# Copying block (1,1) out of PSUM on ScalarE in the pooled and gate quads of a two-layer hybrid backbone

## The chip, the cores and the metric

The kernel runs on one core of a Trainium2 chip. The metric is the device time of one execution in microseconds (us). The engines are called as in the profile: PE (TensorE matmul), PEld (its weight load), DVE (VectorE), ACT (ScalarE), POOL (GpSimd) and SP (SyncE, which issues the DMAs). L1514 is line 1514 of the kernel before.

## What is computed

A latent stream `x` of 1024 tokens of width 1024 goes through two layers and a final RMSNorm. The even layer joins a convolution branch with a bidirectional recurrent branch; the change does not touch it. The odd layer is a multi-scale pooling mixer, and in it lies everything that follows:

```python
def odd_mixer(h, p, on_grid):
    z = h @ p["w_in"]
    u, g = jnp.split(z, [W_POOL], axis=-1)          # W_POOL = 2048
    ...
    d = multiscale_pool(u.reshape(bn * rows, GRID_W, W_POOL)).reshape(bn, n, W_POOL)
    d = d.reshape(bn, n, N_POOL_GROUPS, POOL_GROUP_DIM)
    y = jnp.einsum("bngi,gij->bngj", d, p["w_grp"]).reshape(bn, n, W_POOL) * p["scale"]
    return (y * jax.nn.silu(g)) @ p["w_out"]
```

`multiscale_pool` takes, in rows of 64 tokens, the mean over a window of 2, 4, 8 or 16 tokens (one window for each quarter of the channels) and subtracts the token itself. Since pooling acts along the tokens and `w_grp` along the channels, the kernel folds `w_grp` into the input weights beforehand and pools the product.

## The kernel before

The matrix products of the odd layer are made as **quads**: two row tiles of 128 output channels by two column tiles of 512 tokens, so four blocks (i, h), where i is the row tile and h the column tile. A quad needs seven products in place of eight, in the manner of Strassen. Each product is 12 matmuls (`prod`, L1013): four slices of the contraction by three passes (high weight by high data L1018, high by low L1020, low by high L1021), since each fp32 operand is split into a high and a low part. The seven weight operands of a quad are made while the quad before runs (`wquad_steps`, L979): DVE makes sums of weight blocks, and `split` (L102) makes the high part with a cast on ACT (L103) and then the low part with a subtraction on DVE (L104). In the order of the work they are wq_1, wq_5, wq_6, wq_2, wq_7, wq_3, wq_4; between wq_7 and wq_3 stands a subtraction on DVE (L1006) that wq_3 needs.

`quad` (L1031) uses three accumulators in PSUM, `qa`, `qc` and `qb`, from a pool of four. Its steps:

- p1 into `qa`; ACT copies `qa` to `qb` (L1036); p5 into `qc`, which ACT keeps as a part (L1064); p6 on top of `qb`, kept as a part as well; p2 completes `qa`, which is block (0,0).
- p7 on top of `qb`: with the part of `qc` this gives block (1,1), whose call is `put(1, 1, b, 1)`.
- p3 completes `qc`: with the part of `qb` this gives block (0,1), the second call with part 1, `put(0, 1, c, 1)`.
- p4 completes `qb` as block (1,0). p4 can start only when block (1,1) has been read out of `qb`.

The first argument of `put` is the i of `to_tokens` and `to_gate`, the second is their h. So the call with i = 1 and part 1 is the one that reads `qb` between p7 and p4, and the call with i = 0 and part 1 reads `qc`.

The stage of the change is the loop over pairs of row tiles, m = 0, 2, ..., 14 (808 to 1121 us of the span). Each pass runs a **pooled quad** (its names end in v; blocks go through `to_tokens` into padded token tiles `vp`, which `pool`, L1405, then works on in DVE) and a **gate quad** (names end in g; blocks go through `to_gate` into `y`, get a SiLU on ACT, L1527, and are multiplied with the pooled tokens on DVE, L1557). The window is 4 tokens for m = 0 and 2, 16 for m = 4 and 6, 8 for m = 8 and 10, and 2 for m = 12 and 14; `pool` does one pass of additions (L1420) for each doubling. The blocks of `y` and DVE's sums of them (L962 to L966) are stored to device memory (L1448) and loaded again (L1467) as the operands of the output projection, whose quads end in wo and follow from 1111 us on.

In a pooled quad both blocks with part 1 are read from PSUM by one DVE addition (L1514). In a gate quad this is so too (L1525), but for block (1,1) of the last pair (m = 14): there ACT copies `qb` to `y` (L1523), and DVE adds in place.

The order of instructions on each engine is found by the scheduler, which simulates the program's time; evictions (`put` and L1036) stand under a raised priority. Instructions of one engine run in the order that it wrote down.

Of the kernel before, what the change touches and what calls it, by code (L numbers as in the profile page):

```python
# [56 lines left out]
def body(ctx, tc, xT, ctxT, cc, ccol, modT, modW, win, gw, wout, wu, grp, wg, wo1, small, edge, ident, outT):  # L57
    nc = tc.nc
    mult, add, sub = ALU.mult, ALU.add, ALU.subtract
# [16 lines left out]
    def dtile(name, dt=F32):  # L76
        return dpool.tile([P, S], dt, tag="d", name=name)
# [4 lines left out]
    def ttile(name):  # L82
        return tpool.tile([P, H], F32, tag="t", name=name)
# [73 lines left out]
    def col(o, n=1):  # L157
        return sm[:, o : o + n]
# [73 lines left out]
    def mod_tile(t, l, m, raw, vecs, junk):  # L232
        for i, vec in enumerate(vecs):
            nc.vector.scalar_tensor_tensor(out=junk, in0=raw, scalar=1.0, in1=vec,
                                           op0=mult, op1=mult, accum_out=t[:, i, m : m + 1])
        n = len(vecs)
        v = t[:, :n, m]
        nc.vector.tensor_tensor(out=v, in0=v, in1=col(O_MB + l * 3 * KT + m).to_broadcast([P, n]), op=add)
# [6 lines left out]
    def load_c(i, t, part=slice(0, D)):  # L245
        nc.sync.dma_start(t, cc[i, part].partition_broadcast(P))
        nc.scalar.activation(t, t, AF.Silu)
# [87 lines left out]
    with ExitStack() as sctx:  # L335
# [50 lines left out]
        rows = {}  # L386
# [316 lines left out]
    with ExitStack() as actx:  # L703
# [82 lines left out]
        for j in range(KT):  # L786
# [34 lines left out]
            if state is None:  # L821
                for m in range(3 * KT - 2, 3 * KT):
# [5 lines left out]
                    in1=col(O_MB + 2 * KT, KT), op=add)  # L828
# [144 lines left out]
    def wquad(*args):  # L973
        ops = {}
        for _ in wquad_steps(ops, *args):
            pass
        return tuple(ops[n] for n in range(1, 8))
# [53 lines left out]
    def quad(w, name, ops, put, ahead=None):  # L1031
        p1, p2, p3, p4, p5, p6, p7 = w
        a, c, b = psum(f"qa_{name}"), psum(f"qc_{name}"), psum(f"qb_{name}")
        prod(a, p1, ops["b11"], True, False)
        with tc.high_priority(offset=EVAC):
            evac = nc.scalar.copy(b, a)  # L1036
        prod(c, p5, ops["t1"], True, False)
        with tc.high_priority(offset=EVAC):
            put(1, 1, c, 0)
        prod(b, p6, ops["t2"], False, False)  # L1040
        with tc.high_priority(offset=EVAC):
            put(0, 1, b, 0)
        prod(a, p2, ops["b21"], False, True)
        with tc.high_priority(offset=EVAC):
            put(0, 0, a, None)
        w = None
        if ahead is not None:
            with tc.issue_after(evac.ins):
                w = ahead()
        prod(b, p7, ops["t3"], False, False)  # L1050
        with tc.high_priority(offset=EVAC):
            put(1, 1, b, 1)
        prod(c, p3, ops["b22"], False, True)
        with tc.high_priority(offset=EVAC):
            put(0, 1, c, 1)
        prod(b, p4, ops["t4"], False, True)
        with tc.high_priority(offset=EVAC):
            put(1, 0, b, None)
        return w


    def keep_part(parts, name, i, x):
        parts[i] = ttile(f"s{i}_{name}")
        nc.scalar.copy(parts[i], x)  # L1064
# [292 lines left out]
    def v_weights(m, ring):  # L1357
        return wquad([wfold[(m + i) // 4][(m + i) % 4].rearrange("p k c -> p (k c)") for i in range(2)], f"v{m}", ring)
# [42 lines left out]
    def rows(t):  # L1401
        return t.rearrange("p (r t) -> p r t", t=ROW)


    def pool(m, h, vp):  # L1405
        g = m // 4
        win_ = WINDOWS[g]
        cur = vp
        ww = 1
        while ww < win_:  # L1410
            nxt = atile(f"ws{m}_{h}_{ww}").rearrange("p (r t) -> p r t", t=PW)

            if ww == 1:
                a_, b_ = 1, PW
                o0, o1 = -1, 0
            else:
                hw = ww // 2
                a_, b_ = step + hw, end - hw
                o0, o1 = -hw, hw
            nc.vector.tensor_tensor(out=nxt[:, :, a_:b_], in0=cur[:, :, a_ + o0 : b_ + o0],  # L1420
                                    in1=cur[:, :, a_ + o1 : b_ + o1], op=add)
            step, end = a_, b_
            cur = nxt
            ww *= 2
        hw = win_ // 2

        eo = 16 * g
        left = cur[:, :, PADW : PADW + hw]
        nc.vector.tensor_tensor(out=left, in0=left,
                                in1=eg[:, eo : eo + hw].unsqueeze(1).to_broadcast([P, NR, hw]), op=mult)  # L1430
        if hw > 1:
            right = cur[:, :, PADW + ROW - hw + 1 : PADW + ROW]
            nc.vector.tensor_tensor(out=right, in0=right,
                                    in1=eg[:, eo + 8 : eo + 8 + hw - 1].unsqueeze(1).to_broadcast([P, NR, hw - 1]),
                                    op=mult)
        inner = cur[:, :, PADW : PADW + ROW]
        token = vp[:, :, PADW : PADW + ROW]
        nc.vector.scalar_tensor_tensor(out=token, in0=inner, scalar=1.0 / win_, in1=token, op0=mult, op1=sub)

    NK = 2 * KT  # L1440
# [17 lines left out]
    def y_sums(m):  # L1458
        t = block_sums(*y_blocks(m), vtile(f"yt3_{m}"), nc.vector)
        for name in ("t1", "t2", "t3", "t4"):  # L1460
            y_store(m, name, t[name])
# [14 lines left out]
    def y_operands(part, raws, names=BOPS, alloc=None):  # L1476
        for name in names:
            y_operand(yops[part], part, name, next(raws),
                      alloc or (dtile if name in ("b11", "b21", "t4") else d2tile))
# [17 lines left out]
    for m in range(0, NK, 2):  # L1497
        wv = wv0 if m == 0 else v_weights(m, ring_x)
        if m == 0:
            for i in range(4):  # L1500
                vp = wpool.tile([P, D], F32, tag=("wh", "wl")[i % 2], name=f"vp{i}")[:, : NR * PW]
                vp = vp.rearrange("p (r t) -> p r t", t=PW)
                nc.gpsimd.memset(vp[:, :, 0:PADW], 0.0)
                nc.gpsimd.memset(vp[:, :, PADW + ROW : PW], 0.0)
                vps.append(vp)
        parts = {}

        def to_tokens(i, h, x, part):
            if part is None:
                nc.scalar.copy(token[i][h], rows(x))  # L1510
            elif part == 0:
                keep_part(parts, f"v{m}", i, x)
            else:
                nc.vector.tensor_tensor(out=token[i][h], in0=rows(x), in1=rows(parts[i]), op=add)  # L1514

        def to_gate(i, h, x, part):
            v = ys[m + i][:, HALF[h]]
            if part == 0:
                keep_part(parts, f"g{m}", i, x)
                return  # L1520
            if part == 1:
                if m == NK - 2 and i == 1:
                    nc.scalar.copy(v, x)  # L1523
                    x = v
                nc.vector.tensor_tensor(out=v, in0=x, in1=parts[i], op=add)  # L1525
                x = v
            silu[0] = nc.scalar.activation(v, x, AF.Silu)  # L1527

        token = [[vps[2 * i + h][:, :, PADW : PADW + ROW] for h in range(2)] for i in range(2)]
        quad(wv, f"v{m}", bx, to_tokens)  # L1530
        if m > 0:
            y_sums(m - 2)
        wq = wquad([wg[m + i] for i in range(2)], f"g{m}", ring_x)
        for i in range(2):
            ys[m + i] = dtile(f"y{m + i}")
        if m == 0:
            cL2 = dtile("cL2")
            load_c(0, cL2)
        elif m <= KT:
            n = 2 * KT + m - 2  # L1540
            for q in range(2):
                raw = dtile(f"mod1_{n + q}")
                nc.sync.dma_start(raw, modT[1, n + q])
                mod_tile(m1, 1, n + q, raw, (cL2,), raw)
        if m == NK - 2:
            y_operands(0, iter([dtile] + [xtile] * (4 - 1)), BOPS[:4])
        for i in range(2):
            for h in range(2):
                pool(m + i, h, vps[2 * i + h])
        w = quad(wq, f"g{m}", bx, to_gate, (lambda: wo1_weights(0, 0)) if m == NK - 2 else None)  # L1550
        if m == NK - 2:
            with tc.issue_after(silu[0].ins):
                y_operands(0, iter([xtile] * 7), BOPS[4:])
        for i in range(2):
            for h in range(2):
                gt = rows(ys[m + i][:, HALF[h]])
                nc.vector.scalar_tensor_tensor(out=gt, in0=token[i][h], scalar=col(O_OS + m + i), in1=gt,  # L1557
                                               op0=mult, op1=mult)
        y_keep(m)
# [23 lines left out]
    for m in range(0, KT, 2):  # L1583
        parts = {}
# [111 lines left out]
    m = KT - 4  # L1696
# [213 lines left out]
```

## Time and profile before

| | |
|---|---|
| median of 3 runs | 1291.76 us (1290.92 to 1293.04) |
| the profiled execution's own time | 1292.27 us |
| its span, first to last instruction | 1290.5 us |
| outside the span | 1.8 us |
| mean granted clock of PE | 0.995 |
| busy over the whole span: PE, DVE, ACT | 1264.4, 1133.6, 648.8 us |
| block (1,1) of the pooled quads, L1514 | 8 DVE additions from `qb_v`, 680 ns median |
| block (1,1) of the gate quads, L1525 | 7 DVE additions from `qb_g`, 680 ns median, and 1 from `y`, 683 ns |

A row of the timeline has the start in us from the start of the span, the duration, the engine, the line and operation, the tiles as output<-inputs, and in brackets the idle time ahead of it with what ended it. A row of the waits reads "engine tile line <- what it waited for: us in total, times, longest us". Matmuls are pipelined, so their pace is the distance between starts, not the duration of one.

### The profile page before, as it was taken

The page shows a single profiled execution, that of the slowest core. Times are in us where ns is not written, and L with a number is a line of the kernel's source. Part 1 is how long each engine was busy: PE and PEld are TensorE (multiplying, and loading weights), DVE is VectorE, ACT ScalarE, POOL GpSimd, SP SyncE. Part 2 cuts the span into 40 slices and gives each one's busy share as a digit, 9 for nine tenths or more (in the row PEclk, how much of TensorE's full clock was granted, in tenths as well). Part 3 has the DMA queues.
Part 4 walks back from the last instruction along what each step waited for, and adds up shares of the span by engine and source line. Part 5 has one row for each costly group of instructions (what it writes and reads, how often), then busy time and mean ns, then how long its engine had stood idle before and what let it go on. Part 6 is the DMA issues. An engine that isn't in the chain of part 4 may idle for free.

```text
span 1290.5 us, 16117 instructions
## 1 busy us (share of the span) xinstructions
PE 1264.4 (98%) x5824; PEld 1040.4 (81%) x5824; DVE 1133.6 (88%) x1760; ACT 648.8 (50%) x939; POOL 290.7 (23%) x147
## 2 busy tenths in 40 slices
PE   9999999999999999999999999999999999999996
PEld 7788888888888887888887788787878888788785
DVE  6899999999999999969868959998999987887776
ACT  8555566656656533237434346644333444644542
POOL 0003464436443566434200032000000000000003
PEclk9999999999999999999999999999999999999998
DMA  9961121112111234442418566234333334868633
GB/s 374 396 211 49 42 74 43 64 41 74 57 66 57 82 115 137 143 137 82 163 50 285 173 212 177 92 123 155 117 115 120 115 122 131 298 225 281 212 110 130
DMA packets 78783, 182.33 MB, mean 141 GB/s; under 512 B 7664, under 2 KB 23408, under 8 KB 78704
## 3 DMA queue, kind: packets, MB, share of 16 engines
q1 hardware_dynamic: 70256, 177.12, 40.1%
q10 hardware_dynamic: 8448, 4.20, 1.1%
q8 instruction: 45, 0.74, 0.2%
q14 instruction: 34, 0.28, 0.1%
HBM read 137.24 MB, written 44.04 MB: 140 GB/s over the span
## 4 chain that ended last, share of the span: by engine, by line
PE 49%; DVE 31%; DMA 12%; issue 4%; ACT 3%; POOL 1%; SPq 0%; POOLq 0%; DVEq 0%; ACTq 0%
DVE conv L553 7%; PE wob L553 6%; PE vg L553 5%; PE va L553 5%; PE xb L553 4%; PE fold L123 3%; DVE l L553 3%; PE g L553 3%; DMA yr_t<-y_t 2%; DVE ws L1420 2%; DMA wr_v<-wfold 2%; PE ga L145 2%; PE ga L553 2%; PE ga L144 2%; PE ga L146 2%
## 5 line engine op out<-in xcount | busy, mean ns | idle before, releaser
L553 DVE SCALAR_TENSOR_TENSOR conv<-u,sm,conv 128x505 f32<-128x505 f32 (+6 forms) x224 | 153.5, 744 | 1.0
L1652 POOL TENSOR_TENSOR o<-x,rr 128x256 f32<-128x256 f32 (+1 forms) x10 | 9.9, 1022 | 448.7 <-ACT rr L1652 446.8
L553 ACT ACTIVATE l<-g,sm 128x512 f32<-128x512 f32 (+1 forms) x96 | 58.7, 619 | 57.8 <-PE g L553 57.0
L553 POOL TENSOR_TENSOR l<-l,l 128x1280 f32<-128x1280 f32 x16 | 47.1, 2966 | 25.6 <-DVE conv L553 14.1
L553 PE MATMUL wob<-ybl,wh_wob 128*128 128x512 f32 x128 | 50.2, 392 | 2.3 <-POOL ybl L553 2.3
L123 PE MATMUL fold<-gh,wh_wu 128*128 128x512 f32 x128 | 51.1, 399 | 1.2 <-ACT wh_wu L103 1.2
L103 ACT CAST wq_g<-wr_g 128x512 fp32r<-128x512 f32 x48 | 28.2, 620 | 46.6 <-DMA wr_g<-wg 15.0
L123 PE MATMUL fold<-gh,wl_wu 128*128 128x512 f32 x128 | 50.2, 395 | 0.5 <-DVE wl_wu L104 0.5
L553 PE MATMUL gb<-h0h,wl_gb 128*128 128x512 f32 x128 | 49.9, 390 | 0.3 <-POOL wl_gb L553 0.3
L123 PE MATMUL fold<-gl,wh_wu 128*128 128x512 f32 x128 | 50.1, 391 | 0.0
L553 PE MATMUL va<-h0h,wl_va 128*128 128x512 f32 x128 | 49.9, 390 | 0.1
L553 PE MATMUL vg<-h0h,wl_vg 128*128 128x512 f32 x128 | 49.9, 390 | 0.0
L553 PE MATMUL wob<-ybh,wl_wob 128*128 128x512 f32 x128 | 49.8, 389 | 0.0
L553 PE MATMUL gb<-h0l,wh_gb 128*128 128x512 f32 x128 | 49.8, 389 | 0.0
L553 PE MATMUL gb<-h0h,wh_gb 128*128 128x512 f32 x128 | 49.8, 389 | 0.0
L553 PE MATMUL va<-h0l,wh_va 128*128 128x512 f32 x128 | 49.8, 389 | 0.0
L553 PE MATMUL va<-h0h,wh_va 128*128 128x512 f32 x128 | 49.8, 389 | 0.0
L553 PE MATMUL wob<-ybh,wh_wob 128*128 128x512 f32 x128 | 49.8, 389 | 0.0
L553 PE MATMUL vg<-h0h,wh_vg 128*128 128x512 f32 x128 | 49.8, 389 | 0.0
L553 PE MATMUL vg<-h0l,wh_vg 128*128 128x512 f32 x128 | 49.8, 389 | 0.0
L553 DVE TENSOR_TENSOR_SCAN l<-l,l 128x256 f32<-128x256 f32 (+1 forms) x32 | 48.7, 1522 | 1.1
L553 DVE SCALAR_TENSOR_TENSOR conv<-cL,wsum,conv 128x506 f32<-128x506 f32 (+3 forms) x70 | 48.1, 744 | 0.2
(596 smaller groups left out, 4272.5 us busy)
## 6 DMA issues: line engine op xcount, KB each, us to landing
wr_wu<-wu SPq DMA_DIRECT2D x16, 512.0 KB, 4.2
modw<-modW SPq DMA_DIRECT2D x16, 512.0 KB, 10.2
x_part<-xp SPq DMA_DIRECT2D x32, 256.0 KB, 2.3
mod<-modT SPq DMA_DIRECT2D x32, 256.0 KB, 3.7
wr_v<-wfold SPq DMA_DIRECT2D x16, 512.0 KB, 4.1
wr_g<-wg SPq DMA_DIRECT2D x16, 512.0 KB, 4.8
wr_wo<-wo SPq DMA_DIRECT2D x16, 512.0 KB, 4.5
yr_t<-y_t SPq DMA_DIRECT2D x16, 512.0 KB, 5.8
```

The costliest lines, as they stand in the source:

```text
L103: return (nc.scalar.copy(hi, src), eng.tensor_tensor(out=lo, in0=src, in1=hi.bitcast(F32), op=sub))
L123: m = nc.tensor.matmul(*args, **kw)
L144: mm(ps, hi[:, kc], xh[k][:, cols], start=(k == 0), stop=False)
L145: mm(ps, hi[:, kc], xl[k][:, cols], start=False, stop=False)
L146: mm(ps, lo[:, kc], xh[k][:, cols], start=False, stop=(k == ks - 1))
L553: last[eng] = f(*args, **kw)
L1420: nc.vector.tensor_tensor(out=nxt[:, :, a_:b_], in0=cur[:, :, a_ + o0 : b_ + o0], in1=cur[:, :, a_ + o1 : b_ + o1], op=add)
L1652: tail[eng] = f(*args, **kw)
```

## The change

In `to_tokens`, block (1,1) is now first copied from PSUM to its token tile by ACT; DVE then adds the kept part in place, from SBUF to SBUF. In `to_gate`, the copy that only m = 14 had is made for all pairs. So 15 ACT copies of 128x512 are added (8 pooled, 7 gate), and 15 DVE additions read SBUF where they read PSUM; no DVE instruction is added or removed. The blocks (0,1) are read from PSUM by DVE as before.

```diff
@@ -1510,6 +1510,9 @@
                 nc.scalar.copy(token[i][h], rows(x))
             elif part == 0:
                 keep_part(parts, f"v{m}", i, x)
+            elif i == 1:
+                nc.scalar.copy(token[i][h], rows(x))
+                nc.vector.tensor_tensor(out=token[i][h], in0=token[i][h], in1=rows(parts[i]), op=add)
             else:
                 nc.vector.tensor_tensor(out=token[i][h], in0=rows(x), in1=rows(parts[i]), op=add)
 
@@ -1519,7 +1522,7 @@
                 keep_part(parts, f"g{m}", i, x)
                 return
             if part == 1:
-                if m == NK - 2 and i == 1:
+                if i == 1:
                     nc.scalar.copy(v, x)
                     x = v
                 nc.vector.tensor_tensor(out=v, in0=x, in1=parts[i], op=add)
```

Lines behind it move by three: in the changed kernel the pooled copy is L1514 with its addition L1515, the addition of block (0,1) is L1517, the gate copy is L1526 with its addition L1528, and the SiLU is L1530.

Three places show how the scheduler's order moves. The first is ACT in the pooled quad of m = 6, about 937 to 944 us, where it casts the weights of the gate quad that follows (`wq_g`; `wr_g` and `ws_g` are the raw weights and their sums). Before:

```order
L103 CAST wq_g_5_7828<-wr_g_1_7819 128x512
L103 CAST wq_g_6_7831<-wr_g_0_7817 128x512
L103 CAST wq_g_2_7834<-wr_g_0_7817 128x512
L103 CAST wq_g_7_7837<-ws_g_7824 128x512
L1036 COPY qb_g_7903<-qa_g_7901 128x512
L103 CAST wq_g_3_7841<-wr_g_0_7817 128x512
L103 CAST wq_g_4_7844<-wr_g_1_7819 128x512
```

The same piece of ACT's order in the changed kernel:

```order
L103 CAST wq_g_5_7835<-wr_g_1_7826 128x512
L103 CAST wq_g_6_7838<-wr_g_0_7824 128x512
L103 CAST wq_g_2_7841<-wr_g_0_7824 128x512
L103 CAST wq_g_7_7844<-ws_g_7831 128x512
L1514 COPY vp_6783<-qb_v_7720 128x8x64
L1036 COPY qb_g_7910<-qa_g_7908 128x512
L103 CAST wq_g_3_7848<-wr_g_0_7824 128x512
L103 CAST wq_g_4_7851<-wr_g_1_7826 128x512
```

The new copy stands right behind the cast of wq_7 and ahead of those of wq_3 and wq_4. In 11 of the 15 quads it stands so; in the pooled quads of m = 0, 2 and 14 and in the gate quad of m = 0 it stands one or a few instructions away.

The second place is DVE in the same quad, from the low part of wq_2 on (`y` at L966 is a sum for the stores, `ws_0_4` a step of `pool`). Before:

```order
L104 TENSOR_TENSOR wq_g_2_7834<-wr_g_0_7817,wq_g_2_7834 128x512
L966 TENSOR_TENSOR y_7524<-y_7524,y_7523 128x512
L104 TENSOR_TENSOR wq_g_7_7837<-ws_g_7824,wq_g_7_7837 128x512
L1514 TENSOR_TENSOR vp_6783<-qb_v_7714,s_v_7740 128x8x64
L1420 TENSOR_TENSOR ws_0_4_7861<-ws_0_2_7859 128x8x73
L1514 TENSOR_TENSOR vp_6777<-qc_v_7713,s_v_7754 128x8x64
L1006 TENSOR_TENSOR wr_g_0_7817<-wr_g_0_7817 128x512
```

In the changed kernel DVE has there:

```order
L104 TENSOR_TENSOR wq_g_2_7841<-wr_g_0_7824,wq_g_2_7841 128x512
L104 TENSOR_TENSOR wq_g_7_7844<-ws_g_7831,wq_g_7_7844 128x512
L1420 TENSOR_TENSOR ws_0_4_7868<-ws_0_2_7866 128x8x73
L1517 TENSOR_TENSOR vp_6777<-qc_v_7719,s_v_7760 128x8x64
L1515 TENSOR_TENSOR vp_6783<-vp_6783,s_v_7746 128x8x64
L1006 TENSOR_TENSOR wr_g_0_7824<-wr_g_0_7824 128x512
```

The addition from `qc` now stands ahead of the one for block (1,1), which reads `vp` in SBUF; the sum at L966 has moved to a later place.

The third place is SP behind the last gate quad, about 1116 to 1125 us (`yr_` are loads of the projection's operands, `y_b_1` and `y_t_1` stores of `y` and its sums). Before:

```order
L1467 DMA yr_b_1_9296<-y_b_0_98 128x1024
L1448 DMA y_b_1_100<-y_9083 128x512
L1467 DMA yr_t_0_9302<-y_t_0_99 128x1024
L1448 DMA y_b_1_105<-y_9084 128x512
L1467 DMA yr_t_1_9308<-y_t_0_99 128x1024
L1448 DMA y_t_1_104<-yt_14_9447 128x512
```

And in the changed kernel:

```order
L1467 DMA yr_b_1_9311<-y_b_0_98 128x1024
L1467 DMA yr_t_0_9317<-y_t_0_99 128x1024
L1448 DMA y_b_1_100<-y_9098 128x512
L1467 DMA yr_t_1_9323<-y_t_0_99 128x1024
L1448 DMA y_b_1_105<-y_9099 128x512
L1448 DMA y_t_1_104<-yt_14_9462 128x512
```

The load `yr_t_0` (of operand t4) has changed places with the store `y_b_1_100`, which waits for DVE's product at L1557. POOL's order is the same in both kernels, and on PE the same products stand in a somewhat more regular order.

## The prediction

> **What bounds the kernel now.** I read the page's busy shares first, then the busy time of each engine in stretches of 40 us over the stage, then PE's waits, then PE's timeline at each of them, and last the chain of waits to the end.
>
> ```profile
> PE 1264.4 (98%) x5824; PEld 1040.4 (81%) x5824; DVE 1133.6 (88%) x1760; ACT 648.8 (50%) x939; POOL 290.7 (23%) x147
> ...
> 965.00:1005.00 40.00, 39.88 (x177) 32.69 (x176) 38.17 (x71) 15.36 (x27) 0.00 (x0) 1.00 0.35 112
> 1045.00:1085.00 40.00, 40.00 (x179) 33.10 (x178) 28.69 (x48) 15.63 (x28) 0.00 (x0) 1.00 0.45 149
> sum 320.00, PE 315.06 PEld 257.48 DVE 287.58 ACT 140.26 POOL 0.95; mean PE 39.38 PEld 32.18 DVE 35.95 ACT 17.53 POOL 0.12
> ```
>
> The columns of a stretch are its bounds, its length, and the busy time of PE, PEld, DVE, ACT and POOL. PE bounds the stage (315.06 of 320 us), DVE runs close behind it (38.17 of 40 around m = 6 to 8, with little to give; 28.69 around m = 12), and ACT is idle for more than half. So whatever this change brings must come out of the 4.9 us in which PE is not busy here, and the question is which of them belong to the reader of block (1,1).
>
> ```profile
> PE qb_v L1018 <- DVE vp L1514: 2.0, 2, 1.3
> PE qb_g L1018 <- ACT y L1523: 1.0, 1, 1.0
> ```
>
> From 805 to 1130 us PE waits twice for the pooled addition, and once, at m = 14, for the copy that this kernel has there already. Waits of tenths are not in this list, so I read PE's starts:
>
> ```profile
> 882.97 0.39 PE L1021 MATMUL qa_v<-x_b11h,wq_v 128*128 128x512 f32 x1
> 883.50 0.50 PE L1018 MATMUL qb_g<-x_t4h,wq_g 128*128 128x512 f32 x1
> ...
> 902.48 0.39 PE L1021 MATMUL qa_g<-x_b11h,wq_g 128*128 128x512 f32 x1
> 903.58 0.50 PE L1018 MATMUL qb_v<-x_t4h,wq_v 128*128 128x512 f32 x1 [0.71 <-DVE vp L1514]
> 903.91 0.39 PE L1020 MATMUL qb_v<-x_t4l,wq_v 128*128 128x512 f32 x1
> ...
> 938.40 0.39 PE L1021 MATMUL qb_v<-x_t3h,wq_v 128*128 128x512 f32 x1
> ...
> 941.57 0.39 PE L1021 MATMUL qa_g<-x_b11h,wq_g 128*128 128x512 f32 x1
> 943.22 0.50 PE L1018 MATMUL qb_v<-x_t4h,wq_v 128*128 128x512 f32 x1 [1.26 <-DVE vp L1514]
> 943.56 0.40 PE L1020 MATMUL qb_v<-x_t4l,wq_v 128*128 128x512 f32 x1
> ...
> 1000.24 0.39 PE L1021 MATMUL qa_v<-x_b11h,wq_v 128*128 128x512 f32 x1
> 1000.75 0.50 PE L1018 MATMUL qb_g<-x_t4h,wq_g 128*128 128x512 f32 x1
> ```
>
> The last matmul of p7 at m = 6 starts at 938.40; the two left of p3 and the twelve of the next p1 follow, the last at 941.57: 3.17 / 14 = 0.2267 us is PE's pace. Against it the first matmul of p4 is late by 0.53 - 0.23 = 0.30 (883.50), 1.10 - 0.23 = 0.87 (903.58), 1.65 - 0.23 = 1.42 (943.22) and 0.51 - 0.23 = 0.28 (1000.75). The second matmul behind such a stop comes after 0.33 or 0.34 in place of 0.23, so each costs 0.11 more: 0.41, 0.98, 1.53 and 0.39, **3.31 us in all**. In each the addition on `qb` ends just ahead of p4's start, as here at m = 6 (DVE, then ACT):
>
> ```profile
> 942.48 0.68 DVE L1514 TENSOR_TENSOR vp<-qb_v,s_v 128x512 f32<-128x512 f32 x1
> ```
>
> ```profile
> 938.59 0.62 ACT L103 CAST wq_g<-ws_g 128x512 fp32r<-128x512 f32 x1
> 942.05 0.57 ACT L1036 COPY qb_g<-qa_g 128x512 f32<-128x512 f32 x1 [2.84 <-PE qa_g L1021]
> ```
>
> p7 ended at 938.79 (its last start plus 0.39), but DVE, in arrears, reached the addition at 942.48. ACT was idle from 939.21 for 2.84 us.
>
> **The change part by part.** *The copy on ACT, and the stalls that go.* It stands behind the cast of wq_7. At m = 6 it would run from 939.21 to about 939.8, 2.0 us ahead of the slot of p4 (941.80). Its duration is that of the same copies that the kernel has:
>
> ```profile
> L1510 ACT COPY vp<-qb_v x8: 580/587/588, 835.7 to 1099.0; 128x512 f32<-128x512 f32 x8
> L1523 ACT COPY y<-qb_g x1: 573/573/573, 1116.4 to 1116.4; 128x512 f32<-128x512 f32 x1
> ```
>
> In all four stalled places the new reader is ready in time: 14 matmuls (3.17 us) cover p7's 0.39 us of running out and the 0.58 of the copy. So the stalls go: **-3.31**, bounded by 0 (the copy comes as late as the addition did) and -3.31. The fifteen copies, 15 x 0.58 = 8.7 us of ACT, cost nothing where ACT would wait anyhow:
>
> ```profile
> ACT wq_g L103 <- DVE wr_g L1006: 11.0, 7, 2.8
> ACT wq_v L103 <- DVE wr_v L1006: 5.2, 3, 4.1
> ```
>
> That wait stands just behind the copy's place, between wq_7 and wq_3: on average 1.6 us in the seven pooled quads with weights of a gate quad behind them, and 1.7 us in three of the others. If that cover is gone, a copy delays the cast of wq_3, and DVE behind it, by 0.58.
>
> *DVE's addition from SBUF.* DVE has the same work with another source:
>
> ```profile
> L1525 DVE TENSOR_TENSOR y<-qb_g,s_g x7: 677/680/691, 841.3 to 1074.1; 128x512 f32<-128x512 f32 x7
> L1525 DVE TENSOR_TENSOR y<-y,s_g x1: 683/683/683, 1118.7 to 1118.7; 128x512 f32<-128x512 f32 x1
> ```
>
> 680 ns from PSUM, 683 ns from SBUF at m = 14: 15 x 0.003 = 0.05 us, taken as **0** (from -0.2 to +0.2 by the spread of these rows).
>
> [...]
>
> *What is late next.* With PE up to 3.31 us ahead, its other readers matter. The block from `qc` must be read before the next p5; the closest cases are in the gate quads, here that of m = 6:
>
> ```profile
> 962.87 0.68 DVE L1525 TENSOR_TENSOR y<-qc_g,s_g 128x512 f32<-128x512 f32 x1
> ```
>
> ```profile
> 965.56 0.39 PE L1018 MATMUL qc_v<-x_t1h,wq_v 128*128 128x512 f32 x1
> ```
>
> It ends 2.01 us ahead of p5 (965.56 - 963.55). PE would arrive 2.92 us earlier (three of the stalls), while this addition comes about 0.6 us earlier, since it now goes ahead of the one on block (1,1). That leaves PE late by about 0.3: no more than some 2.6 us of the gain is through here if DVE doesn't move, and the fourth stall's 0.39 may come on top.
>
> *How much of it reaches the end.* By the chain of waits the end does not hang on PE after 1074 us, but on DVE and then on loads:
>
> ```profile
> 1070.98 0.68 DVE L104 TENSOR_TENSOR wq_v<-ws_v,wq_v 128x512 fp32r<-128x512 f32 x1
> 1074.07 0.69 DVE L1525 TENSOR_TENSOR y<-qb_g,s_g 128x512 f32<-128x512 f32 x1 [2.40 <-PE qb_g L1021]
> ```
>
> ```profile
> 1074.07 1.29 DVE y L1525 x2
> 1075.36 0.61 DVE wq_v L104
> 1075.98 3.61 DMA wr_g<-wg
> ...
> 1118.15 0.67 DVE y L1557
> 1118.85 0.32 SPq L1448
> 1119.26 5.78 DMA yr_t<-y_t
> ```
>
> ```profile
> 1128.12 0.51 PE L1018 MATMUL qc_wo<-y_b22h,wq_wo 128*128 128x512 f32 x1
> 1129.55 0.50 PE L1018 MATMUL qb_wo<-y_t3h,wq_wo 128*128 128x512 f32 x1 [0.92 <-ACT s_wo L1064]
> ```
>
> At m = 12 DVE waits 2.40 us for p7. It can't take more than that from a PE that comes earlier, so the chain moves by **-2.40** at most. DVE now asks for `qc` first, whose p3 ends 2 x 0.2267 = 0.45 us behind p7; with PE 2.6 to 2.9 earlier that is 1074.07 + 0.45 - 2.6 = 1071.9 at worst, against 1071.67 at which DVE is free, so it costs 0 to 0.2. The floor of this term is 0: if DVE's or the loads' own pace sets 1075.98.
>
> *SP near the end.* The load of t4 was issued at 1119.26, behind a store that waited for the product of 1118.15. Put ahead of it, it can go up to 1.9 us earlier, right behind the b22 load. The operand of t4 is cast on ACT ahead of the copy s_wo for which PE stops at 1129.55, for 1.43 - 0.23 = 1.20 us. The gain lies between 0 (the load shares the queues' bandwidth with the b22 load, and both are needed) and -1.2; I take **-0.5**, nearer to nothing, since 5.78 us is a load slowed by others.
>
> Sum: -2.40 + 0 - 0.50 = -2.90. The profiled execution took 1292.27 us, 0.51 above the median of 1291.76; 1292.27 - 2.90 = 1289.37 there, and **1288.9** as a median.
>
> **The rivals.** *DVE's pace takes the gain back.* For it: DVE has 38.17 of 40 us busy where the stalls are, and at m = 14 ACT, DVE and loads set the pace, so an earlier PE may only wait longer at 1117 and 1129 us. Against it: the list of PE's waits names no weights of a pooled or gate quad, and DVE itself waits 2.40 for PE at m = 12. The edit then gives 0 to 2.4: about 1289.3 to 1291.8, in the middle 1290.5.
>
> *The copy stands in ACT's way (slower).* Place: between the casts of wq_7 and wq_3, and in the gate quads ahead of the SiLU. A copy whose p7 is not done holds the casts behind it, and DVE waits for casts already:
>
> ```profile
> DVE wq_v L104 <- ACT wq_v L103: 8.0, 8, 1.6
> DVE wq_g L104 <- ACT wq_g L103: 6.7, 6, 1.7
> ```
>
> Price: 15 x 0.58 = 8.7 us, less the 3.31 of the stalls and DVE's 2.40 to spare, so +3.0: 1294.8. It decides from the tenth copy on that really delays DVE ((3.31 + 2.40) / 0.58 = 9.8). For it: at m = 14 the copy that is there made PE wait 1.0. Against it: the 16.2 us of ACT's waits for L1006, in ten quads, and 140 us of work in 320.
>
> [...]
>
> *The edit does not act:* the order would have to put the copy late, and it stands right behind wq_7 in 11 of 15 quads; the stalls would stay, 1291.8.
>
> **How the numbers follow.** Forecast (1288.9, its own range 1287.8 to 1289.8): 0.50. Gain taken back: 0.32. Copy in the way: 0.14. No effect: 0.04. The lower end is both gains in full: 1291.76 - 3.31 - 1.2 = 1287.25, so 1287.2. The upper end takes in the second and fourth case and most of the third up to 1294.0. A measurement of this kernel tells about 0.2%, 2.6 us, from no change, so faster means below 1289.2 and slower above 1294.3. Of the forecast some four fifths lie below 1289.2, of the rival of DVE's pace a fifth: 0.40 + 0.06 = 0.46 faster. Slower is 0.11, four fifths of the copy's rival. The rest, 0.43, is the same within 0.2%.
>
> **What would show it.** PE's starts at p4 of m = 2 (gate), 4, 6 (pooled) and 8 (gate) come 0.23 behind the matmul before; PE's waits for vp are gone; the copies take 0.57 to 0.59 and end over 1 us ahead of p4; DVE's additions from SBUF stay at 0.68; DVE's wait at 1074 us shrinks from 2.40 to nearly nothing; the last load of t4 is issued nearer to b22's. A wait of PE for L1517 or for the `qc` addition at m = 4 to 8 would show that DVE has the gain. DVE waits for wq_3 and wq_4 that grow from 14.7 us to over 20 would show the slower rival. The forecast is wrong if the chain behind 1080 us hangs on loads that do not come earlier.

## The result, and the profile after

The changed kernel takes **1288.16 us** (median of 10 runs, 1284.27 to 1292.63) against 1291.58 us (median of 10 runs, 1288.59 to 1293.48): a ratio of **0.9971, interval 0.9958 to 0.9983**. The medians differ by 3.42 us; 2.90 were forecast.

The profiled execution has a span of 1282.7 us against 1290.5, so 7.8 us less, and the first thing to read is where these lie, for they aren't all the change's. The first matmul of the first gate quad starts at 818.69 us before and at 814.61 after: 4.1 us are gained ahead of the stage, where the order on every engine is the same in both kernels. The first matmul of the output projection comes at 1112.41 and at 1104.87, so **the stage between these marks takes 293.72 us before and 290.26 after, 3.46 us less**. From there to the end, which I call the tail, it is 178.07 and 177.80. These are the three windows that I use below; the stage's are, before and then after (bounds, length, busy time of PE, PEld, DVE, ACT, POOL, then clock and DMA):

```profile
818.69:1112.41 293.72, 291.42 (x1279) 239.50 (x1279) 261.44 (x459) 122.05 (x209) 0.46 (x4) 1.00 0.39 129
```

```profile
814.61:1104.87 290.26, 290.19 (x1280) 239.90 (x1279) 262.10 (x460) 127.75 (x224) 0.48 (x4) 1.00 0.39 131
```

PE is now busy in all but 0.07 us. DVE has the same work as before (262.10 against 261.44) in a shorter stage. ACT is busy 5.7 us more, less than the 8.8 of fifteen copies at 0.585 us: neighbours on ACT overlap in the profile, at m = 6 by 0.09 us (the cast ends at 934.47, the copy starts at 934.38). PE's waits from 805 to 1130 us are down to one row, the copy at m = 14 that was there before:

```profile
PE qb_g L1018 <- ACT y L1526: 1.3, 1, 1.3
```

At the place of the largest stop, p4 of the pooled quad of m = 6, PE's timeline now shows no gap (1.65 us between these two starts before):

```profile
936.00 0.39 PE L1021 MATMUL qa_g<-x_b11h,wq_g 128*128 128x512 f32 x1
936.23 0.39 PE L1018 MATMUL qb_v<-x_t4h,wq_v 128*128 128x512 f32 x1
```

ACT and DVE there:

```profile
933.86 0.61 ACT L103 CAST wq_g<-ws_g 128x512 fp32r<-128x512 f32 x1
934.38 0.58 ACT L1514 COPY vp<-qb_v 128x512 f32<-128x512 f32 x1
936.48 0.57 ACT L1036 COPY qb_g<-qa_g 128x512 f32<-128x512 f32 x1 [1.53 <-PE qa_g L1021]
```

```profile
937.82 0.68 DVE L1517 TENSOR_TENSOR vp<-qc_v,s_v 128x512 f32<-128x512 f32 x1
938.42 0.68 DVE L1515 TENSOR_TENSOR vp<-vp,s_v 128x512 f32<-128x512 f32 x1
```

The copy ends at 934.96, 1.3 us ahead of p4. DVE has not become faster here: it comes to block (1,1) at 938.42, 2.2 us after p4 has begun. Only PE doesn't wait for it there any more. The copies and additions cost what the rows of before said (ACT 587 and 585 ns, DVE from SBUF 678 and 680):

```profile
L1514 ACT COPY vp<-qb_v x8: 576/587/590, 823.0 to 1087.1; 128x512 f32<-128x512 f32 x8
L1515 DVE TENSOR_TENSOR vp<-vp,s_v x8: 677/678/682, 825.8 to 1087.7; 128x512 f32<-128x512 f32 x8
...
L1526 ACT COPY y<-qb_g x8: 577/585/589, 836.2 to 1108.5; 128x512 f32<-128x512 f32 x8
L1528 DVE TENSOR_TENSOR y<-y,s_g x8: 677/680/687, 838.1 to 1110.6; 128x512 f32<-128x512 f32 x8
```

### The profile page after: what moved, and what is told of

The parts are those of the page before. It is cut to its first block, busy times and chain, and to the rows that moved or that the text cites. A ratio compares the mean times of both kernels' runs of the same rounds, so it can differ in the third digit from the quotient of the medians.

```text
span 1282.7 us, 16124 instructions
## 1 busy us (share of the span) xinstructions
PE 1261.9 (98%) x5824; PEld 1040.9 (81%) x5824; DVE 1132.6 (88%) x1760; ACT 654.7 (51%) x954; POOL 289.7 (23%) x147
## 4 chain that ended last, share of the span: by engine, by line
PE 64%; DVE 23%; DMA 8%; issue 2%; ACT 2%; POOL 1%; SPq 0%; POOLq 0%; DVEq 0%; ACTq 0%
DVE conv L553 7%; PE fold L123 6%; PE wob L553 6%; PE vg L553 5%; PE va L553 5%; PE xb L553 4%; DVE l L553 3%; PE g L553 3%; PE ga L553 2%; PE ga L146 2%; PE ga L145 2%; PE ga L144 2%; DMA yr_b<-y_b 2%; PE xbc L553 2%; PE qb_g L1021 1%
## 5 line engine op out<-in xcount | busy, mean ns | idle before, releaser
L103 ACT CAST wq_g<-wr_g 128x512 fp32r<-128x512 f32 x48 | 28.2, 621 | 52.9 <-DVE wr_g L998 21.6
```

The lines of the kernel that those rows point to most:

```text
L103: return (nc.scalar.copy(hi, src), eng.tensor_tensor(out=lo, in0=src, in1=hi.bitcast(F32), op=sub))
```

## The experiments

Two theories stand against each other. **The stops:** PE loses time only where the block that p4 waits for is read by an engine in arrears; the change takes DVE's arrears out of that path. **DVE's pace:** DVE sets the stage, and an earlier PE meets it again at the next quad. A third, **ACT's queue**, arose from the trace after. ACT's waits for DVE's addition at the SiLU were 12.8 us in six times before and 4.7 in three after (first before, then after):

```profile
ACT y L1527 <- DVE y L1525: 12.8, 6, 3.6
```

```profile
ACT y L1530 <- DVE y L1528: 4.7, 3, 3.5
```

So the gain might come from casts that are no longer held behind the SiLU. The measure is the length of the stage in the profile, with PE's stops in it; each stop is given as its gap against PE's pace of 0.2267 us, and the matmul behind it adds 0.11. The times of whole runs of one kernel spread by 4 to 11 us, so they can tell the ends apart but not each term.

**The spread first.** The kernel before and the changed kernel, each profiled once more.

> The kernel before once more, for one profile. Between the two profiles 4.1 us of the 7.8 us by which the span fell lie ahead of the changed stage, where both kernels have the same order on every engine. Theory that this part is the spread of the executions (waits for loads at 687 to 755 and at 809 us): the first matmul of the first gate quad lies anywhere from 814 to 820 us here too, and the stage again takes 293.5 to 294 us with the four stops. Rival, the change shifts it: it lies at 818.5 to 819 us as before.

> The changed kernel once more, for one profile: the spread of the stage. Two profiles of the kernel before gave 293.72 and 295.59 us for the stage, with four and with five stops. Theory: in the changed kernel nothing of the stage waits for DVE's additions, so the stage is again 290.2 to 290.6 us, whatever the parts ahead and behind take (first gate quad at 814 to 820 us, tail 177 to 181). Rival: the first profile was a lucky execution, and stops of 0.3 to 1.5 us for the copy or for qc appear: stage 291 to 293.

Measured: before again, the first gate quad at 818.98 us, the stage **295.59** us, with stops of 0.45, 0.72, 1.81, 0.28, a new one of 0.66 us at m = 14 (pooled), a small one of 0.09 at m = 4 (gate), and 0.36 us at the closing mark itself, where PE waited for a weight of the projection; a tail of 179.28. After again, the first gate quad at 816.06, the stage **290.07**, with none, a tail of 177.93:

```profile
816.06:1106.14 290.08, 290.08 (x1280) 239.70 (x1278) 261.84 (x459) 127.35 (x224) 0.48 (x4) 1.00 0.39 131
```

Over the thirteen profiles of this study, all with the same order ahead of the stage, the first gate quad lies anywhere from 814.61 to 819.27 us. So the 4.1 us ahead of the stage are no effect that these runs show to be the change's; the stage's gain is, 3.5 us in the first pair of profiles and 5.5 in the second, of which 0.4 are the wait at the closing mark. Before, the stage has a spread of its own: the same places stop PE by 0.72 or 0.87 and by 1.42 or 1.81 us. After, it stands at PE's own time in both profiles. I had expected 293.5 to 294 us in the first of these, and four stops; there were five clear ones.

**One kind of quad alone.** The copy in the pooled quads only:

```diff
-                if i == 1:
+                if m == NK - 2 and i == 1:
                     nc.scalar.copy(v, x)
```

> The ACT copy in the eight pooled quads alone; the gate quads as before. The stage is measured from the first matmul of the first gate quad to the first of the output projection: 293.72 us before, 290.26 with the whole change. Theory of the stops: PE loses only where DVE's addition on qb is in arrears, so the pooled stops of 0.98 and 1.53 us go and the two gate stops stay or grow by what DVE lacks: stage 291.0 to 292.4, ratio to before about 0.9985. Rival, DVE's pace: PE meets DVE again at the next gate quad and the stops move there (slack of 0.43 us at m = 4 and 6): stage 293 to 293.7, ratio 0.9995 to 1. Rival, ACT's queue: the gain comes from the SiLU that no longer holds the casts; since the gate quads are as before, stage 293.7.

Measured: stage 291.65 us, ratio 0.9988 (0.9973 to 1.0003). The copy in the gate quads only:

```diff
-            elif i == 1:
-                nc.scalar.copy(token[i][h], rows(x))
-                nc.vector.tensor_tensor(out=token[i][h], in0=token[i][h], in1=rows(parts[i]), op=add)
```

> The ACT copy in the gate quads alone; the pooled quads as before. Theory of the stops: the two gate stops, 0.41 and 0.39 us, go; the pooled ones of 0.98 and 1.53 stay, and grow where PE comes earlier: stage 292.9 to 293.7, ratio about 0.9995. Rival, ACT's queue (the SiLU of block (1,1) waited 12.8 us for DVE's addition before and 4.7 with the whole change, and the casts behind it with it): DVE's waits for casts fall from 14.7 to about 10 us here too, DVE catches up and the pooled stops shrink with it: stage 290.5 to 292, ratio about 0.998.

Measured: stage 293.07 us, ratio 0.9997 (0.9983 to 1.001). What is left of PE's stops, first with the pooled quads' copies, then with the gate quads':

```profile
997.79 0.39 PE L1021 MATMUL qa_v<-x_b11h,wq_v 128*128 128x512 f32 x1
999.27 0.50 PE L1018 MATMUL qb_g<-x_t4h,wq_g 128*128 128x512 f32 x1 [1.09 <-DVE y L1528]
```

```profile
901.38 0.39 PE L1021 MATMUL qa_g<-x_b11h,wq_g 128*128 128x512 f32 x1
903.02 0.50 PE L1018 MATMUL qb_v<-x_t4h,wq_v 128*128 128x512 f32 x1 [1.26 <-DVE vp L1514]
...
941.01 0.39 PE L1021 MATMUL qa_g<-x_b11h,wq_g 128*128 128x512 f32 x1
942.49 0.50 PE L1018 MATMUL qb_v<-x_t4h,wq_v 128*128 128x512 f32 x1 [1.10 <-DVE vp L1514]
```

With the pooled copies the pooled stops are gone, and the gate stop of m = 8 has grown from 0.28 to 1.25: 1.25 + 0.11 = 1.36, and 291.65 - 290.26 = 1.39. With the gate copies the pooled stops stand at 1.41 and 1.25: with 0.22 they make 2.88, and 293.07 - 290.26 = 2.81. The stage is PE's own time plus the stops, to 0.1 us, in both. ACT's queue falls: with the gate copies ACT's waits at the SiLU do go down to 4.4 us, but DVE's waits for ACT's casts come to 16.8 us (14.7 before; about 10 was expected), and the pooled stops stay. DVE's pace falls in its strong form (293 to 293.7 with the pooled copies), though the grown stop at m = 8 is what it says in small.

**The four places alone.** The copy only where PE stopped in the profile of before:

```diff
-            elif i == 1:
+            elif i == 1 and m in (4, 6):
...
-                if i == 1:
+                if i == 1 and m in (2, 8, NK - 2):
```

> The ACT copy only where PE stopped: pooled quads of m = 4 and 6, gate quads of m = 2 and 8 (and m = 14, which had it). Theory of the stops, simple form: the whole 3.31 us go, stage 290.3 to 290.6, ratio about 0.997. Theory of the stops with DVE's reach: PE is earlier by up to 3 us at the other quads, where DVE's addition on qb had only 0.43 to 0.69 us to spare (gate m = 4 and 6, pooled m = 8 and 10); new stops there, stage 291.5 to 293, ratio 0.998 to 0.9995.

Measured: stage 292.00 us, ratio 0.9984 (0.997 to 0.9999). The four stops are gone and two others are there, of 0.71 and 0.39 us, in quads that had 0.44 and 0.59 us to spare before:

```profile
918.99 0.39 PE L1021 MATMUL qa_v<-x_b11h,wq_v 128*128 128x512 f32 x1
919.93 0.50 PE L1018 MATMUL qb_g<-x_t4h,wq_g 128*128 128x512 f32 x1 [0.55 <-DVE y L1528]
...
1015.29 0.39 PE L1021 MATMUL qa_g<-x_b11h,wq_g 128*128 128x512 f32 x1
1015.91 0.50 PE L1018 MATMUL qb_v<-x_t4h,wq_v 128*128 128x512 f32 x1 [0.24 <-DVE vp L1517]
```

So the copies at places without a stop do work too: they keep an earlier PE from running into DVE. That was the second form of the theory.

**The engine.** The whole change, with DVE as the one that copies:

```diff
-                nc.scalar.copy(token[i][h], rows(x))
+                nc.vector.tensor_copy(token[i][h], rows(x))
...
-                    nc.scalar.copy(v, x)
+                    (nc.scalar.copy if m == NK - 2 else nc.vector.tensor_copy)(v, x)
```

> The whole change, but the copy out of PSUM is made by DVE and not by ACT (m = 14 of the gate quads stays with ACT). DVE then has 14 instructions more, about 0.6 us each, 8 to 9 us in the stage, and PE waits for DVE as before. Theory of the stops: what helps is that the reader is not the engine in arrears; here PE's stops come back and are larger: stage 294 to 299, ratio 1.000 to 1.004. Rival: what helps is the order of DVE's work (block (0,1) first, the sums of L966 later), which this kernel keeps: stage 290.3 to 292, ratio about 0.998.

Measured: stage 292.99 us, ratio 0.9999 (0.9989 to 1.001), with stops of 0.79 (m = 4, for the copy) and 1.38 (m = 8, for the block in `qc`). DVE's busy time in the stage:

```profile
818.49:1111.47 292.98, 291.07 (x1279) 239.41 (x1279) 269.55 (x474) 122.54 (x209) 0.48 (x4) 1.00 0.39 128
```

With DVE as the reader the gain is gone. That speaks against the order of DVE's work as the cause, but it is no clean test of it: the scheduler made another order for this kernel, in which DVE reads block (1,1) ahead of block (0,1) in ten of fifteen quads. Against that rival stands also the timeline of the changed kernel: there DVE reaches block (1,1) of m = 6 only 2.2 us after p4 has begun. And I missed as well: fifteen more DVE instructions (8 pooled, 7 gate; the expectation counts one too few) should have lengthened the stage to 294 us or more, and it is 0.7 us shorter than before. DVE took 8.1 us more work (269.55 against 261.44) out of its idle time. It is late at some places and idle at others; 89% busy over the stage did not mean that it had nothing to give.

**The place in ACT's order.** Every copy made twice, the second right behind the first in the program:

```diff
                 nc.scalar.copy(token[i][h], rows(x))
+                nc.scalar.copy(token[i][h], rows(x))
...
                     nc.scalar.copy(v, x)
+                    nc.scalar.copy(v, x)
```

> The whole change, and every copy of block (1,1) on ACT made twice, one behind the other (16 ACT instructions more, 0.58 us each, 9.3 us). It prices the copy on ACT. Theory of the stops (ACT has cover, and the copy stood 1.3 to 2.4 us ahead of p4): p4 still finds its accumulator free nearly everywhere, stage 290.3 to 291.2 us (290.26 with the single copy), only the stop at m = 14 grows by about 0.6; ratio 0.997 to 0.998. Rival, the copy in ACT's way: casts and DVE behind them come later by some of the 9.3 us, stage 292 to 296, ratio 0.999 to 1.002.

Measured: stage **297.50** us, ratio **1.0028 (1.0011 to 1.0044)**, slower than before, though ACT is only about half busy (137.79 of 292.23 us with as many copies in the next kernel). PE stops for the second copy in three pooled quads (1.17, 1.61 and 2.19 us). ACT at the second of these:

```profile
898.99 0.59 ACT L1514 COPY vp<-qb_v 128x512 f32<-128x512 f32 x1 [0.33 <-PE qb_v L1021]
901.90 1.14 ACT L103 CAST wq_g<-wr_g 128x512 fp32r<-128x512 f32 x2 [2.32 <-DVE wr_g L1006]
902.95 0.58 ACT L1515 COPY vp<-qb_v 128x512 f32<-128x512 f32 x1
```

The scheduler put the casts of wq_3 and wq_4 between the two copies. These wait 2.32 us for DVE, the second copy stands behind them, and PE behind that. That points at the place in the order, and not at the 0.58 us. (The stage holds another 1.6 us of a slower clock behind the stop of 2.19; the last section has it.) So the copies were doubled once more, with the casts held behind both:

```diff
+        with ExitStack() as octx:
+            if name[0] in "vg" and taken[0] is not None:
+                octx.enter_context(tc.issue_after(taken[0].ins))
             ops[3] = op(a12, 3)
...
                 nc.scalar.copy(token[i][h], rows(x))
+                taken[0] = nc.scalar.copy(token[i][h], rows(x))
...
```

> Every copy of block (1,1) on ACT made twice, and both kept ahead of the casts of wq_3 and wq_4 (where the copies were doubled without that, the second one of the pooled quads came behind these casts in ACT's order, and PE stopped for it by 1.17, 1.61 and 2.19 us). It prices ACT's time for the copy alone: 16 x 0.58 = 9.3 us more on ACT. Theory of the place in the queue: with the place kept, ACT's time costs nearly nothing: stage 290.3 to 291.5 us, ratio to before 0.997 to 0.9985. Rival, ACT's time: casts come later and DVE with them, stage 294 to 298 as with the copies doubled freely (297.5), ratio 1.001 to 1.003.

Measured: stage 292.23 us, ratio 0.9976 (0.9962 to 0.9991). ACT has 10.0 us more than with single copies:

```profile
819.02:1111.25 292.23, 290.80 (x1278) 239.67 (x1279) 263.19 (x461) 137.79 (x240) 0.47 (x4) 1.00 0.38 130
```

The stage is 0.7 us longer than I gave it. Its one large stop, 1.23 us, is in the pooled quad of m = 2, where the second copy comes behind casts up to wq_7 that wait for DVE: the place again. The same doubled copies, then, cost 7.2 us of stage against the single ones where the scheduler put them, and 2.0 where the casts of wq_3 and wq_4 came behind them. And the other way round, one copy, held behind the cast of wq_4 (`behind` sets the order on ACT alone, `cast` is the last cast made):

```diff
+        if name[0] in "vg" and taken[0] is not None:
+            behind(taken[0].ins, cast[0].ins)
...
-                nc.scalar.copy(token[i][h], rows(x))
+                taken[0] = nc.scalar.copy(token[i][h], rows(x))
...
```

> The whole change with one copy for each block, but ACT's order holds it behind the casts of wq_3 and wq_4 of the next weights, which wait for DVE (L1006). Theory of the place in the queue: ACT then is as late as DVE, PE stops for the copy in the pooled quads and gate quads of m = 2 to 10 where DVE is in arrears, and these stops are longer than before by the two casts and the copy: stage 295 to 302 us, ratio to before 1.001 to 1.007. Rival, the engine alone counts: stage 290.3 to 291, ratio 0.997 to 0.998.

Measured: stage 294.62 us, ratio 1.0013 (0.9995 to 1.003). The gain is gone, as the theory has it, but just short of the 295 that I gave as its least, and the stops sit elsewhere than I said. At m = 8 ACT reaches the copy 6 us after p7:

```profile
980.69 0.57 ACT L1045 COPY qb_g<-qa_g 128x512 f32<-128x512 f32 x1 [2.55 <-PE qa_g L1030]
982.68 1.14 ACT L103 CAST wq_g<-wr_g 128x512 fp32r<-128x512 f32 x2 [1.42 <-DVE wr_g L1013]
983.73 0.58 ACT L1523 COPY vp<-qb_v 128x512 f32<-128x512 f32 x1
```

```profile
982.19 0.47 PE L1027 MATMUL qc_g<-x_t1h,wq_g 128*128 128x512 f32 x1 [1.59 <-DVE vp L1526]
```

The scheduler, which knows that order, put p5 of the next quad ahead of p4 here, so PE doesn't stop for the copy; at p5 it stops for 1.75 us, for `qc`, which DVE reads. With p4 moved behind it, p5 has lost the 2.7 us of cover that p4 gave it, and DVE's arrears come through at that block. The only large stop for the copy itself is 0.44 us, in the pooled quad of m = 14. So this run shows that the gain goes with the place, but most of what PE loses in it, it loses at `qc`.

**The last stop.** At m = 14 the copy is late behind ACT's casts of loaded operands (p7 ended at 1104.58, the copy began at 1108.51), so two kernels try to get its 1.45 us. Without that one copy:

```diff
-                if i == 1:
+                if i == 1 and m < NK - 2:
```

> The whole change without the copy at m = 14 of the gate quads, the one that the kernel before has too: there DVE adds from PSUM. With the change PE's last stop of that stage, 1.45 us, is for this copy, which ACT reaches 3.9 us after p7. Theory that any copy behind ACT's casts of loaded operands is late: the stop changes to a wait for DVE, which is just as late there (it took y_b21 and wq_wo until 1109.4): stop 0.7 to 2 us, the same within noise as the whole change, ratio 0.996 to 0.998. Rival, the copy itself is to blame: the stop goes, 1.4 us less, ratio about 0.9960. The stage before it stays at 290.3 in both.

Measured: stage 290.45, stop 1.38 us for DVE's addition in its place, ratio 0.9982 (0.9968 to 0.9996). The copy isn't to blame. With the load and casts of b21 asked for later:

```diff
-            y_operands(0, iter([dtile] + [xtile] * (4 - 1)), BOPS[:4])
+            y_operands(0, iter([dtile] + [xtile] * (4 - 1)), BOPS[:3])
...
-                y_operands(0, iter([xtile] * 7), BOPS[4:])
+                y_operands(0, iter([xtile] * 7), BOPS[3:])
```

> The whole change, and the load and the casts of operand b21 of the output projection asked for behind the last SiLU of the gate quad of m = 14 and not ahead of that quad, so that ACT's copy of block (1,1) no longer stands behind the two casts of y_b21 that waited for their loads. Theory: the stop of 1.45 us at m = 14 goes; if y_b21 is in time for its product about 18 us later, 1.0 to 1.5 us of it reach the end, ratio 0.9955 to 0.9965. Rival: the loads set the end behind 1105 us (the chain of waits runs through them), and PE stops later by as much for y_b21, y_t3 or y_t4: ratio 0.997 to 0.999.

Measured: stage 290.55 us, ratio 0.9993 (0.9981 to 1.0006). The stop at m = 14 is gone, and PE stops later for more: 0.76 us at 1126.76 for y_b22, and here:

```profile
1134.72 0.47 PE L1018 MATMUL qc_wo<-y_t1h,wq_wo 128*128 128x512 f32 x1 [1.54 <-DVE xp L1575]
```

The tail is 181.97 us against 177.80; some 1.6 us of that are the slower clock of the last section. In this run the stop taken away at m = 14 came back as waits for loaded operands and for DVE. Neither beats the changed kernel.

## Why the prediction was right, and where a step failed

*The four stops.* Right, and the whole of the gain. 3.31 us were counted from PE's starts; the stage lost 3.46. The kernels with one kind of quad show the same sum, PE's own time of about 290.2 us plus the stops, to 0.1 us; the one with four places shows it to 0.4 (292.00 less 0.71, 0.39 and 0.11 for each of three matmuls behind a stop is 290.6).

*ACT's copies at no cost.* Right for the place that the order gave them, at 0.585 us apiece: none of them is on PE's path in the stage. DVE's waits for ACT's casts, which were to grow from 14.7 us to over 20 if the copies stood in the way, fell to 9.4:

```profile
DVE wq_g L104 <- ACT wq_g L103: 5.1, 7, 1.5
DVE wq_v L104 <- ACT wq_v L103: 4.3, 6, 1.8
```

The condition that the prediction named, the wait for L1006 just behind, is what decides: with the copy moved behind that wait the gain is gone (294.62, though mostly by way of `qc`), and a second copy there costs more than the first one brings (297.50 against 292.23 ahead of it). The slower rival was at the right place, then, with the wrong mechanism. It let the copy delay the casts; in the runs it was the casts that delayed the copy (by their wait of 2.32 us for DVE in the kernel with doubled copies, 1.42 in the one with the late copy).

*DVE from SBUF.* Right: 678 and 680 ns, the medians of eight instructions each, against 680 from PSUM.

*The block in `qc`.* The 0.3 us that were to be lost there did not appear in the two profiles of the changed kernel. At the place that the prediction reckoned with, the gate quad of m = 6, DVE's reading of it ended at 957.23 and p5 began at 957.99: 0.76 us were left (0.62 in the second profile). Closest was the pooled quad of m = 6, with 938.50 and 938.95: 0.45 us (0.25 in the second). In the kernel with b21 late PE did stop there, for 0.54 us. It is the next thing to be late.

*How much reaches the end: the step that failed.* The prediction capped the gain at 2.40 us, by DVE's wait for p7 at m = 12. After the change DVE still waits there, as long as before and the 0.45 us of p3 on top:

```profile
1063.45 0.68 DVE L104 TENSOR_TENSOR wq_v<-ws_v,wq_v 128x512 fp32r<-128x512 f32 x1
1066.99 0.69 DVE L1528 TENSOR_TENSOR y<-qc_g,s_g 128x512 f32<-128x512 f32 x1 [2.85 <-PE qc_g L1021]
```

DVE is free at 1064.13, which is 249.52 us after the first gate quad; before, 1071.66 was 252.97 after it. So DVE itself came 3.45 us earlier, with PE. It could, because it had more idle time than that one wait: 32.3 us in the stage before (293.72 - 261.44), 28.2 after. The kernel with DVE's copies showed the same reserve. A wait at one place bounds what an engine can gain only if the engine is at work all the way up to it. The lists of waits point at the one that gave way: up to 1071.66 and 1064.13 DVE did the same work (232.66 and 232.75 us), and its waits for ACT's casts fell from 13.7 to 8.5 us, while its waits for loads and stores went from 5.1 to 6.1. Over the whole stage they fell from 14.8 to 8.7 in the second pair of profiles. Why the casts came earlier is open.

*SP near the end.* The load of t4 now goes at 1109.30, ahead of the store (1110.75), and the stop of 1.20 us that it ended in is gone. Whether 0.5 us of it reached the end isn't shown: the tail is 0.27 us shorter in the one pair of profiles and 1.35 in the other, from the same two orders, and over the thirteen profiles, of other orders too, it lies between 174.75 and 184.97. PE has other stops in the tail, which vary as much. These, for y_b22 and y_t4 of the second half, make 2.27 us of waits; in the kernel before, the same three make 1.70, and in the second pair of profiles it is the other way round (2.43 in four waits before, 1.71 after):

```profile
1205.50 0.50 PE L1020 MATMUL qc_wo<-y_b22l,wq_wo 128*128 128x512 f32 x1 [0.76 <-DVE y_b22l L104]
1207.71 0.51 PE L1018 MATMUL qb_wo<-y_t4h,wq_wo 128*128 128x512 f32 x1 [0.76 <-ACT y_t4h L103]
1208.97 0.50 PE L1020 MATMUL qb_wo<-y_t4l,wq_wo 128*128 128x512 f32 x1 [0.75 <-DVE y_t4l L104]
```

So the sum came out near (-2.90 against -3.42) with its first term 1.06 us too small (2.40 for the 3.46 of the stage) by a cap that wasn't there, and its last one not shown. That it came so near is in part luck: the two errors work against each other, and by the interval of the ratio the gain itself is known only as 2.2 to 5.4 us.

## What to carry to other kernels

When a saturated engine waits for one accumulator to be read, hand the reading to an engine that stands idle at that moment, even if the reading then takes an instruction more (here fifteen copies of 0.585 us, for a stage shorter by 3.46): the work may stay late as long as the accumulator comes free (at m = 6 DVE came 2.2 us after p4 had begun). Look at what stands ahead of the reader in its engine's order, since an idle engine whose queue waits for the late one comes late with it (ACT's casts waited 2.32 us for DVE, and PE stopped 1.61 us for the copy behind them); hold the reader ahead of such waits if the scheduler doesn't. And protect the neighbours too, for here an earlier PE ran into the same engine at places that had only 0.44 and 0.59 us to spare.

## What the runs showed of the hardware

A stop of PE of about 2 us cost more than itself in some executions. In the kernel with doubled copies PE waited 2.02 us, and the third matmul behind it and the seven after that started 0.43 us apart in place of 0.23:

```profile
1020.36 0.50 PE L1018 MATMUL qb_v<-x_t4h,wq_v 128*128 128x512 f32 x1 [2.02 <-ACT vp L1515]
1020.70 0.40 PE L1020 MATMUL qb_v<-x_t4l,wq_v 128*128 128x512 f32 x1
1020.93 0.46 PE L1021 MATMUL qb_v<-x_t4h,wq_v 128*128 128x512 f32 x1
1021.18 0.63 PE L1018 MATMUL qb_v<-x_t4h,wq_v 128*128 128x512 f32 x1
1021.61 0.63 PE L1020 MATMUL qb_v<-x_t4l,wq_v 128*128 128x512 f32 x1
```

The granted clock over the next 4 us was 0.58:

```profile
1020.50:1024.50 4.00, 4.00 (x11) 3.20 (x12) 3.96 (x7) 0.29 (x1) 0.00 (x0) 0.58 0.62 174
```

That is 8 x 0.2 = 1.6 us beside the stop's 2.2. The same followed a wait of 2.00 us at 717 us in the kernel before (clock 0.57). But the length of the wait alone doesn't decide it: in the kernel with the copies doubled and held ahead, a longer wait at the same place was not followed by it (the mean clock of that execution is 0.997, against 0.995 in the kernel before),

```profile
717.32 0.50 PE L1025 MATMUL qc_woa<-ya_t1h,wq_woa 128*128 128x512 f32 x1 [2.07 <-DVE wq_woa L104]
```

nor were the waits of 1.26 us before (clock 1.00 over 925 to 965 us) and of 1.65 us in the second profile of that kernel (mean clock 0.996), both at m = 6. In the kernel with b21 late, the slower clock came behind the wait of 1.54 us at 1134.72: 0.50 over eight matmuls, from 1136.90 to 1140.00 us, so about 1.6 us. What decides is open here.
